# A two-block transformer kernel on one core: a fixed opening order with strided copies on three engines, and a norm summed by matmuls with its residual scaling put off

## Chip, cores and metric

One core of one Trainium2 chip. The metric is the device time of one execution in microseconds, as the median over several runs. The kernel is given all inputs in device memory and writes one 512 x 1024 output.

## The reference, cut to what matters

A first block (one Conformer-like layer with sparse attention) is followed by a second block of two attention layers. 512 tokens, width 1024, fp32 throughout. The change touches three places: the first block's first norm and the projections that follow it, the hand-over between the blocks (the first block's last sum and final norm, the second block's first norm), and the latent inputs and dense attention of the second block's first layer.

```python
def first_block(x, ...):
    h = rms_norm(x, norm1_g[l])                       # the opening
    proj = h @ w_in[l]                                # q, k_c, v_c, k_s, v_s, k_w, v_w, gates, ...
    ...                                               # compress(): windows of 32 tokens, step 16, of k_c and v_c
    x = x + (g_a * y_attn + g_b * y_conv) @ w_out[l]
    x = x + conv_ffn(rms_norm(x, norm2_g[l]), ...)    # its last product is ... @ w_down
    return rms_norm(x, final_g)                       # the residual x of the second block

def second_block(x, c, ...):
    for layer in range(2):
        shift, scale, gate = split(silu(c) @ ada_w[layer] + ada_b[layer])
        h = rms_norm_2(x, norm_w[layer]) * (1 + scale) + shift
        y = even_mixer(h, ...) if layer == 0 else odd_mixer(h, ...)
        x = x + gate * y
    return rms_norm_2(x, final_norm)

def even_mixer(h, ...):
    qa, ka, va, ga, cq, ckv, kr, gb = split(h @ w_in)
    oa = dense_gqa_attention(rope(rms_norm_2(qa)), rope(rms_norm_2(ka)), va)   # 8 heads, 512 x 512 scores
    cq, ckv = rms_norm_2(cq), rms_norm_2(ckv)                                  # the latent inputs
    ob = mla_attention(...)
    return concat([oa * silu(ga), ob * silu(gb)]) @ w_out
```

## The kernel before, in words

The residual is held transposed, as eight tiles X[k] of 128 channels x 512 tokens. Every fp32 operand of a large product is split into a rounded high part and a low remainder, and `mm3` (L121 to L126) makes three matmuls for each of them: L124 low by high, L125 high by low, L126 high by high. A weight tile is loaded by `wload` (L100): a DMA, ACT's copy to the high part (L110) and a subtraction for the low part (L111) on POOL or DVE. Results go to PSUM banks of four groups: "pg" and "ps" (two banks each), "pt" (three) and "po" (one). `gemm_bank` gives a pg bank, `wide_bank` pg and ps in turn. A tile framework adds the semaphores and a scheduler sets each engine's order from the dependences; where `in_order(engine)` stands around code, that engine takes those instructions in the order in which they are written.

Opening (L303 to L424). For each of the eight tiles ACT makes the high part, scaled by the gain (L305), and DVE the low part. Two key/value tiles pkv (24 matmuls each) follow, and eight squares on ACT with DVE adds between them (`Squares`, L193), summed over the partitions by eight fp32 matmuls with a one-column operand (L224, L225). `newton` makes the reciprocal root in eight small DVE steps (L164 to L173), and `row_bcast` spreads it over the partitions by four matmuls (L184), copied to R1 by DVE (L190). `windows` (L328) multiplies a pkv tile by R1 (L330), splits it (L152 on ACT, L153 on DVE) and lays it out as overlapping windows with 16 strided copies of 64 partitions x 8 x 31 elements, source step 16: eight of the high part on DVE (L347), eight of the low part on ACT (L349). It runs twice, for ZK and ZV. Two more tiles, pkb, are computed in between, multiplied by R1 (L402) and stacked by `stack_k` (L241 and L243 on ACT, L242 and L244 on DVE). Then `natural` (L405) computes four 280-column tiles wv in pg banks, each evacuated by ACT with the per-row factor (L417), and the query and compression products follow.

Hand-over (L755 to L806, L895 to L898). The last down product comes in two token halves th, of 256 columns: for each of the eight row tiles m a product of 12 matmuls in a wide bank, an add into X[m] on DVE (L792), and two squares on ACT: of X and of X times the final gain, each kind accumulated on DVE (L207, L210). At the end of a half: eight fp32 sum matmuls (L224, L225), Newton on four columns, a broadcast (L184), and for each k the modulated input by `modulated`: L772 on DVE, L773 on ACT, L774 on DVE. The split of w_kv and w_qa begins after the first half. After both halves, POOL turns X into the second block's residual with two instructions for each tile and half: times r0 (L897), times the final gain (L898). The program has them after the q/k/v products; POOL takes them where the scheduler lets them.

Latent inputs (`latent_inputs`, L881): four 416-column tiles in pg banks, each with its own squares and its own Newton before ACT's scaled copies can free the bank. Dense attention (`dense_scores`, L916): for each of eight heads, four score tiles, reduce_max on DVE (L924), Exp on ACT (L926), reciprocal on DVE (L927), and the scaling of P on POOL (L928); transposes of P and the product with the values follow. The gate and latent products of the loop take their weights through ACT L110 and POOL L111.

## Time and profile before

| | us |
|---|---|
| median of 3 runs (lowest, highest) | 1329.89 (1329.7, 1336.98) |
| profiled execution, its own time | 1332.08 |
| span of that execution | 1330.3 |
| PE busy in the span | 1259.4 |
| DVE, POOL, ACT busy | 930.5, 722.3, 707.0 |

The profile was taken from one execution; its own time is 1.8 us over its span and 2.2 us over the median of the runs. Times in the rows below are microseconds from the start of the span, unless marked ns. Engines: PE = TensorE matmuls, PEld = its weight loads (which run beside matmuls), DVE = VectorE, ACT = ScalarE, POOL = GpSimd, SP = SyncE. L12 is line 12 of the kernel. PEclk is the granted clock of TensorE as a share of full speed. A bracket behind a row is the idle time of the engine before it, and what ended it. An fp32 matmul leaves two records. Tile names are by kind (x, h, p, ps), without their numbers.

### The profile page before, as it was taken

The numbers are of one execution on the slowest core, as the hardware profiler recorded it, in microseconds if no ns is written. First come the engines' busy times: TensorE is split into PE (matmuls) and PEld (weight loads), VectorE is DVE, ScalarE is ACT, GpSimd is POOL, SyncE is SP. The second block draws the span as 40 slices with busy tenths as digits, with TensorE's granted clock in tenths as the row PEclk, the third lists the DMA queues.
The fourth block names the chain that finished last, engine by engine and source line by source line (L and its number), as shares of the span: only waits on it lengthen the run. The fifth ranks groups of instructions, "written<-read, shape, count | busy, mean of one in ns | idle before, by whom it ended". The sixth has DMA issues, their size and how long they took to land. (4 is left out here: it accounts for less than half of the span.)

```text
span 1330.3 us, 19304 instructions
## 1 busy us (share of the span) xinstructions
PE 1259.4 (95%) x6337; PEld 1044.6 (79%) x6337; DVE 930.5 (70%) x2042; ACT 707.0 (53%) x1497; POOL 722.3 (54%) x699
## 2 busy tenths in 40 slices
PE   7889999899999999999999979899999989999997
PEld 5778877688878888888888778878777788888886
DVE  7555666886644777754778788686788786666565
ACT  5736678434443444423443353386666645776554
POOL 4157786844644666655664554345445432767542
PEclk9899999999999999999999989999999989999998
DMA  7131112232333455555554601211111111111221
GB/s 228 40 100 48 49 50 65 89 101 88 119 111 95 159 170 163 165 187 164 170 158 131 221 24 39 62 46 46 45 55 48 33 56 48 60 59 52 70 72 64
DMA packets 71973, 124.75 MB, mean 94 GB/s; under 512 B 8257, under 2 KB 17345, under 8 KB 71873
## 3 DMA queue, kind: packets, MB, share of 16 engines
q1 hardware_dynamic: 71872, 123.52, 29.7%
q8 instruction: 50, 0.82, 0.2%
q14 instruction: 51, 0.41, 0.1%
HBM read 121.39 MB, written 2.10 MB: 93 GB/s over the span
## 5 line engine op out<-in xcount | busy, mean ns | idle before, releaser
L111 POOL TENSOR_TENSOR wl<-wr,wh 128x512 fp32r<-128x512 f32 (+2 forms) x215 | 286.3, 1333 | 283.4 <-ACT wh L110 224.5
L124 PE MATMUL pg<-h,wl 128*128 128x512 f32 x628 | 249.1, 397 | 3.2 <-POOL wl L111 3.1
L125 PE MATMUL pg<-h,wh 128*128 128x512 f32 x628 | 247.0, 393 | 0.0
L126 PE MATMUL pg<-h,wh 128*128 128x512 f32 x628 | 246.9, 393 | 0.0
L110 ACT ACTIVATE wh<-wr 128x512 fp32r<-128x512 f32 (+2 forms) x215 | 132.5, 618 | 157.3 <-PE pg L126 79.3
L124 PEld LDWEIGHTS pg<-h,wl 128*128 128x128 f32 x628 | 118.3, 188 | 26.9 <-POOL wl L111 4.5
L126 PEld LDWEIGHTS pg<-h,wh 128*128 128x128 f32 x628 | 118.4, 189 | 22.5
L125 PEld LDWEIGHTS pg<-h,wh 128*128 128x128 f32 x628 | 118.5, 189 | 22.4 <-issue 0.7
L111 POOL TENSOR_TENSOR m<-t,m 128x512 fp32r<-128x512 f32 (+1 forms) x67 | 87.9, 1312 | 75.2 <-ACT m L110 66.8
L286 PE MATMUL po<-t,h 128*128 128x512 f32 (+3 forms) x384 | 111.1, 365 | 7.5 <-DVE t L281 3.6
L281 DVE TENSOR_TENSOR t<-pt,t 128x512 fp32r<-128x512 f32 (+1 forms) x160 | 97.6, 631 | 28.3 <-ACT t L280 27.2
L124 PE MATMUL ps<-h,wl 128*128 128x512 f32 x260 | 103.7, 399 | 5.7 <-POOL wl L111 3.8
L125 PE MATMUL ps<-h,wh 128*128 128x512 f32 x260 | 102.6, 395 | 0.5 <-DVE h L156 0.5
L126 PE MATMUL ps<-h,wh 128*128 128x512 f32 x260 | 102.7, 395 | 0.0
L280 ACT ACTIVATE t<-pt 128x512 fp32r<-128x512 f32 (+1 forms) x160 | 84.4, 552 | 20.0 <-PE pt L276 19.3
L286 PEld LDWEIGHTS po<-t,h 128*128 128x128 f32 x384 | 65.7, 188 | 33.5 <-ACT t L280 16.4
L276 PE MATMUL pt<-k,p 128*128 128x128 f32 x576 | 86.6, 273 | 0.9 <-POOL p L928 0.7
L276 PEld LDWEIGHTS pt<-k,p 128*128 128x128 f32 x576 | 69.4, 140 | 13.7 <-POOL p L928 3.5
L928 POOL TENSOR_SCALAR p<-p,s 128x512 f32<-128x512 f32 x64 | 44.9, 704 | 62.9 <-DVE s L927 62.3
L702 DVE CUSTOM_DVE_ANT_0 b<-b,z 128x512 f32<-128x512 f32 x48 | 75.7, 1578 | 0.6 <-DMA b<-ada_t 0.6
L110 ACT ACTIVATE m<-t 128x512 fp32r<-128x512 f32 (+2 forms) x78 | 46.8, 602 | 40.3 <-PE ps L124 12.2
L124 PEld LDWEIGHTS ps<-h,wl 128*128 128x128 f32 x260 | 49.7, 191 | 17.8 <-POOL wl L111 4.8
(376 smaller groups left out, 3113.2 us busy)
## 6 DMA issues: line engine op xcount, KB each, us to landing
b<-ada_t SPq DMA_DIRECT2D x48, 256.0 KB, 3.1
z<-ada_t SPq DMA_DIRECT2D x48, 256.0 KB, 3.0
t<-w_up SPq DMA_DIRECT2D x44, 256.0 KB, 2.8
wr<-w_up SPq DMA_DIRECT2D x44, 256.0 KB, 2.7
wr<-w_g SPq DMA_DIRECT2D x32, 256.0 KB, 2.6
t<-w_dn SPq DMA_DIRECT2D x23, 256.0 KB, 2.8
wr<-w_br SPq DMA_DIRECT2D x16, 256.0 KB, 2.6
wr<-w_gt SPq DMA_DIRECT2D x16, 256.0 KB, 2.8
```

Source lines behind the costliest of these rows:

```text
L110: A.activation(hi[:, :z], raw[:, :z], AF.Copy)
L111: eng.tensor_sub(lo[:, :z], raw[:, :z], f(hi[:, :z]))
L124: PE.matmul(ps, ll, rh, start=start and i == 0, stop=False)
L125: PE.matmul(ps, lh, rl, start=False, stop=False)
L126: PE.matmul(ps, lh, rh, start=False, stop=stop and i == n - 1)
L276: PE.transpose(ps[:, o:o + 128], src, ident)
L280: evac[:] = [A.activation(hi[:, :n], ps[:, :n], AF.Copy)]
L281: evac.append(V.tensor_sub(lo[:, :n], ps[:, :n], f(hi[:, :n])))
L286: PE.matmul(o[:, a:b], v, t[:, pa:pa + b - a], start=start and z == 0, stop=stop and z == 1)
L702: V.tensor_tensor_reduce(out=raw, in0=raw, in1=CA[z], op0=OP.mult, op1=OP.add, scale=1.0, scalar=0.0, accum_out=MA[l][:, z, m:m + 1])
L928: G.tensor_scalar(p, p, sm[:, 1:2], 0.0, op0=OP.mult, op1=OP.add)
```

## The change

1. Opening. The high parts of all eight tiles, with their weights', now stand on ACT before the squares, in fixed order. PE's order is fixed as well: both pkv products, half of the first pkb product, the norm's sums (in a pt bank), its other half, the broadcast of R1, the second pkb product. Both pkv tiles are multiplied by R1 at once. The strided copies of each window set go four to DVE, six to ACT and six to POOL (before: eight, eight, none), and the products of pkb with R1 stand between the two window sets. The wv tiles take wide banks.
2. Second block's first norm. A class `Weighted` replaces the two `Squares` of a half: one square per row tile on ACT and no DVE adds, then, for both 128-token parts, an fp32 matmul of the squares with two columns (one, and the squared gain), accumulated in the "po" bank over the eight row tiles.
3. The factor on the queries, q3, moves from DVE to POOL.
4. The latent inputs take wide banks, and one Newton on eight columns serves all four tiles.
5. The residual's scaling moves from the hand-over into the dense loop: after each head's last scaling of P, the four POOL instructions of one tile X[k].

```diff
-        def sums(self):
-            st = new("ps")
+        def sums(self, bank="ps"):
+            st = new(bank)
...
+    class Weighted:
+        def __init__(self, a, w):
+            self.c, self.w, self.n, self.st = slice(a, a + 256), w, 0, new("po")
+        def add(self, src):
+            t = new("p")
+            A.activation(t[:, self.c], src[:, self.c], AF.Square)
+            k = self.n
+            for i in range(2):
+                PE.matmul(self.st[:, 2 * i:2 * i + 2], t[:, self.c][:, i * 128:(i + 1) * 128], self.w[:, k, :],
+                          start=k == 0 and i == 0, stop=k == KT - 1, skip_group_check=True)
+            self.n += 1
...
+    with in_order("PE"):
+        for b in range(2):
+            mm3(pkv[b], w0[8 * b:8 * b + 8], xg)
+        mm3(pkb[0], wk[0][:4], xg[:4], True, False)
+        r1 = rsqrt(total.sums("pt"), 1.0 / D, EPS)
+        mm3(pkb[0], wk[0][4:], xg[4:], False, True)
+        R1 = to_sbuf(row_bcast(r1, "pt"))
+        pkb.append(new("ps"))
+        mm3(pkb[1], wk[1], xg)
...
-                        if zz is zh:
+                        if zz is zh and o == 0:
                             V.tensor_copy(dst, src)
+                        elif zz is zh or g + o == 2:
+                            A.activation(dst, src, AF.Copy)
                         else:
-                            A.activation(dst, src, AF.Copy)
+                            G.tensor_copy(dst, src)
...
-        ps = natural(wv, xg, 280, i)
+        ps = natural(wv, xg, 280, i, wide_bank)
...
     def down(th, m, ps, c):
+        if m == 0:
+            sums.append(Weighted(256 * th, fg2))
         V.tensor_add(X[m][:, c], X[m][:, c], ps)
-        sums[th][0].add(X[m])
-        sums[th][1].add(X[m], cv("fg", m))
+        sums[th].add(X[m])
...
-                V.tensor_tensor(q3, q3, r[:, 0:8].to_broadcast([128, 8, 64]), op=OP.mult)
+                G.tensor_tensor(q3, q3, r[:, 0:8].to_broadcast([128, 8, 64]), op=OP.mult)
...
-    for r0, c in xr:
-        for k in range(KT):
-            G.tensor_mul(X[k][:, c], X[k][:, c], r0)
-            G.tensor_scalar(X[k][:, c], X[k][:, c], cv("fg", k), 0.0, op0=OP.mult, op1=OP.add)
-    for i in range(4):
-        latent_inputs(wc, i)
+    def latent_inputs(w):
+        ss = new("s", (128, 16))[:, 0:8]
+        banks = []
+        for i in range(4):
+            ps = natural(w, H, 416, i, wide_bank)
...
+        rc = rsqrt(ss, 1.0, EPS)
+        for i, ps in enumerate(banks):
...
+    def residual(k):
+        with tc.issue_after(getattr(scaled[0], "ins", scaled[0])):
+            for r0, c in xr:
+                G.tensor_mul(X[k][:, c], X[k][:, c], r0)
+                G.tensor_scalar(X[k][:, c], X[k][:, c], cv("fg", k), 0.0, op0=OP.mult, op1=OP.add)
...
         dense_output(h, P, [v[:, h // 4, :] for v in VA])
+        residual(h)
```

The order of the instructions at three places follows, before and after; the line numbers are each kernel's own.

ACT in the opening, before, from the split of the first pkv tile (p99) on: L349 are the strided copies, L361 a compression weight.

```order
L152 ACTIVATE p98_368<-p97_366 128x512
L349 ACTIVATE h101_373<-p99_369 64x8x31 x4
L349 ACTIVATE h103_387<-p99_369 64x8x31 x4
L152 ACTIVATE p105_402<-p104_400 128x512
L110 ACTIVATE wh141_651<-t140_650 128x512
L361 ACTIVATE wh149_691<-t148_690 128x2x128
L349 ACTIVATE h108_407<-p106_403 64x8x31 x4
L349 ACTIVATE h110_421<-p106_403 64x8x31 x4
```

The same place on ACT after the change (L376 are the strided copies, L390 the compression weights, L257 the first of the stack copies).

```order
L152 ACTIVATE p101_420<-p72_360 128x512
L376 ACTIVATE h103_424<-p101_420 64x8x31 x2
L376 ACTIVATE h105_438<-p101_420 64x8x31
L376 ACTIVATE h104_425<-p102_421 64x8x31
L376 ACTIVATE h105_438<-p101_420 64x8x31
L376 ACTIVATE h106_439<-p102_421 64x8x31
L390 ACTIVATE wh149_691<-t148_690 128x2x128
L390 ACTIVATE wl151_700<-wr150_699 128x2x128
L257 ACTIVATE h115_488<-p107_452 64x512
```

Six of the sixteen copies of a set stay on ACT between the split and the stack copies; six more are POOL's and four DVE's.

DVE where the first half's norm is applied while the second half's products arrive, before: L792 is the add into a row tile x, L774 the low part of a modulated input, L207 and L210 the adds of squares, L111 a weight split.

```order
L774 SCALAR_TENSOR_TENSOR h1889_7747<-p1887_7745,k1089_4351,h1888_7746 128x256
L792 TENSOR_TENSOR x7_112<-x7_112,pg1943_7893 128x256
L774 SCALAR_TENSOR_TENSOR h1892_7753<-p1890_7751,k1089_4351,h1891_7752 128x256
L207 TENSOR_TENSOR z1940_7887<-p1933_7849,p1936_7867 128x256
L774 SCALAR_TENSOR_TENSOR h1895_7759<-p1893_7757,k1089_4351,h1894_7758 128x256
L207 TENSOR_TENSOR z1942_7891<-p1934_7851,p1937_7869 128x256
L792 TENSOR_TENSOR x8_113<-x8_113,ps1946_7913 128x256
```

The same place after the change: L802 is the low part, L825 the add into a row tile.

```order
L802 SCALAR_TENSOR_TENSOR h1879_7727<-p1877_7725,k1089_4351,h1878_7726 128x256
L825 TENSOR_TENSOR x7_112<-x7_112,pg1929_7870 128x256
L802 SCALAR_TENSOR_TENSOR h1882_7733<-p1880_7731,k1089_4351,h1881_7732 128x256
L825 TENSOR_TENSOR x8_113<-x8_113,ps1931_7888 128x256
L802 SCALAR_TENSOR_TENSOR h1885_7739<-p1883_7737,k1089_4351,h1884_7738 128x256
L825 TENSOR_TENSOR x9_114<-x9_114,pg1933_7906 128x256
```

The adds of squares are gone from between; the add into x7 still stands behind the sixth of the eight low parts.

POOL in the dense loop before, around the end of one head's scalings (L928 scales P, L111 is a weight split for a gate product).

```order
L928 TENSOR_SCALAR p2125_8784<-p2125_8784,s2124_8782 128x512
L928 TENSOR_SCALAR p2129_8794<-p2129_8794,s2128_8792 128x512
L111 TENSOR_TENSOR wl2274_9277<-wr2272_9275,wh2273_9276 128x512
L928 TENSOR_SCALAR p2133_8804<-p2133_8804,s2132_8802 128x512
L928 TENSOR_SCALAR p2168_8943<-p2168_8943,s2167_8941 128x512
```

POOL in the dense loop after the change, at the end of another head's scalings (L960 scales P, L970 and L971 are the residual's two steps on tile x4, L111 is a weight split for a gate product).

```order
L960 TENSOR_SCALAR p2100_8690<-p2100_8690,s2099_8688 128x512
L970 TENSOR_TENSOR x4_109<-x4_109,r1861_7693 128x256
L970 TENSOR_TENSOR x4_109<-x4_109,r1944_7980 128x256
L971 TENSOR_SCALAR x4_109<-x4_109,k2_107 128x256 x2
L111 TENSOR_TENSOR wl2241_9175<-wr2239_9173,wh2240_9174 128x512
L960 TENSOR_SCALAR p2135_8833<-p2135_8833,s2134_8831 128x512
```

Four instructions now stand between a head's last P scaling and what follows it, a weight split here; before, scalings and splits alone made up the queue.

## Rows read from the trace of the kernel before

**Rows 1.** The page's first section: engines' busy time.
```profile
PE 1259.4 (95%) x6337; PEld 1044.6 (79%) x6337; DVE 930.5 (70%) x2042; ACT 707.0 (53%) x1497; POOL 722.3 (54%) x699
```

**Rows 2.** Windows: us, busy PE, PEld, DVE, ACT, POOL, PEclk, DMA, GB/s.
```profile
51.27:55.63 4.36, 4.36 (x18) 4.36 (x19) 2.13 (x5) 2.19 (x8) 1.60 (x2) 0.50 0.31 90
...
59.57:110.00 50.43, 45.93 (x245) 38.63 (x244) 29.19 (x79) 23.33 (x58) 25.45 (x28) 0.97 0.24 77
...
783.55:799.50 15.95, 8.66 (x40) 8.16 (x39) 15.95 (x25) 10.77 (x26) 12.03 (x14) 0.59 0.09 23
...
842.42:866.58 24.16, 18.34 (x91) 16.74 (x90) 14.34 (x61) 9.35 (x28) 2.58 (x2) 0.93 0.10 33
...
866.58:1000.00 133.42, 127.67 (x642) 99.76 (x640) 101.40 (x217) 94.41 (x209) 66.89 (x74) 1.00 0.15 46
```

**Rows 3.** Timeline of PE, opening: start, duration, instruction, idle before.
```profile
28.08 1.68 PE L184 MATMUL pt<-k,s 128*128 128x128 f32 x8 [2.27 <-DVE s L173]
...
39.57 0.29 PE L124 MATMUL pg<-m,h 128*128 128x280 f32 x1
...
51.27 0.60 PE L124 MATMUL pg<-m,h 128*128 128x280 f32 x1 [5.40 <-ACT p L417]
...
59.57 0.39 PE L124 MATMUL pg<-h,wl 128*128 128x512 f32 x1
```

**Rows 4.** Groups by form, 20 to 60 us: busy, mean ns, idle.
```profile
L349 ACT ACTIVATE h<-p 64x248 fp32r<-64x248 f32 x16 | 10.2, 638 | 1.6 <-DVE p L153 1.4
...
L347 DVE CAST h<-p 64x248 fp32r<-64x248 f32 x16 | 7.1, 441 | 0.2
...
L243 ACT ACTIVATE h<-p 64x512 fp32r<-64x512 f32 x4 | 2.5, 628 | 0.1
```

**Rows 5.** Timeline of ACT, opening.
```profile
33.71 5.17 ACT L349 ACTIVATE h<-p 64x248 fp32r<-64x248 f32 x8 [1.44 <-DVE p L153]
...
50.72 0.49 ACT L417 ACTIVATE p<-pg,s 128x280 f32<-128x280 f32 x1
```

**Rows 6.** Timeline of DVE, opening.
```profile
30.52 0.69 DVE L330 TENSOR_TENSOR p<-pg,r 128x512 f32<-128x512 f32 x1
```

**Rows 7.** Timeline of PE, hand-over and latent inputs.
```profile
787.21 0.58 PE L124 MATMUL pg<-h,h 128*128 128x256 f32 x1 [3.38 <-DVE x L792]
...
794.05 0.58 PE L124 MATMUL pg<-m,h 128*128 128x256 f32 x1 [3.91 <-DVE x L792]
...
846.85 0.43 PE L124 MATMUL pg<-m,h 128*128 128x416 f32 x1 [4.42 <-DVE p L833]
...
866.16 0.66 PE L906 MATMUL pt<-k,h 128*128 128x128 f32 x4 [1.40 <-ACT h L243]
```

**Rows 8.** Groups by form, 758 to 866 us.
```profile
L897 POOL TENSOR_TENSOR x<-x,r 128x256 f32<-128x256 f32 x16 | 12.7, 793 | 11.8 <-DVE p L772 11.8
...
L898 POOL TENSOR_SCALAR x<-x,k 128x256 f32<-128x256 f32 x16 | 9.0, 561 | 1.6
...
L210 DVE TENSOR_TENSOR z<-z,p 128x256 f32<-128x256 f32 x20 | 10.8, 562 | 1.3 <-ACT p L217 1.1
...
L224 PE MATMUL ps<-k,z 128*128 128x1 f32 x16 | 2.8, 246 | 0.0
```

**Rows 9.** Timeline of DVE, hand-over.
```profile
779.71 0.48 DVE L774 SCALAR_TENSOR_TENSOR h<-p,k,h 128x256 fp32r<-128x256 f32 x1
...
781.84 1.02 DVE L774 SCALAR_TENSOR_TENSOR h<-p,k,h 128x256 fp32r<-128x256 f32 x1
```

**Rows 10.** Timeline of POOL, hand-over.
```profile
781.84 0.74 POOL L897 TENSOR_TENSOR x<-x,r 128x256 f32<-128x256 f32 x1
```

**Rows 11.** The page's section of groups: two groups of POOL.
```profile
L111 POOL TENSOR_TENSOR wl<-wr,wh 128x512 fp32r<-128x512 f32 (+2 forms) x215 | 286.3, 1333 | 283.4 <-ACT wh L110 224.5
...
L928 POOL TENSOR_SCALAR p<-p,s 128x512 f32<-128x512 f32 x64 | 44.9, 704 | 62.9 <-DVE s L927 62.3
```

More of the change, by code (lines that the diff above doesn't have):

```diff
@@ L325, in gemm, with windows @@
         return ps
-    def windows(ps, pe):
-        t = new("p")
-        V.tensor_mul(t, ps, R1)
+    def windows(t, pe):
         th, tl = split(t, p="p")
@@ L387, in build @@
     KB = []
-    wk = [wsplit(I["w_q"][2 + b], KT, 128) for b in range(2)]
     wv = wsplit(I["w_v"], KT, 280, ("m", "h"))
@@ L395, in build @@
     w2k, w2v = [(w2h[:, i:i + 64], w2l[:, i:i + 64]) for i in (0, 64)]
-    ZK = windows(pkv[0], cv("pek", 0, 16))
-    ZV = windows(pkv[1], cv("pev", 0, 16))
+    ZK = windows(tkv[0], cv("pek", 0, 16))
+    tkb = []
     for b in range(2):
-        ps = new("ps")
-        mm3(ps, wk[b], xg)
-        t = new("p")
-        V.tensor_mul(t, ps, R1)
+        tkb.append(new("p"))
+        V.tensor_mul(tkb[b], pkb[b], R1)
+    ZV = windows(tkv[1], cv("pev", 0, 16))
+    for t in tkb:
         KB.append([stack_k(t, 0), stack_k(t, 64)])
@@ L788, in build @@
     H = [None] * KT
-    sums = [[Squares(256 * th, 256 * th + 256) for _ in range(2)] for th in range(2)]
+    fg2 = new("k", (128, KT, 2), tag="fg2")
+    V.memset(fg2[:, :, 0], 1.0)
+    V.tensor_mul(fg2[:, :, 1], cv("fg", 0, 8), cv("fg", 0, 8))
+    sums = []
     def down(th, m, ps, c):
+        if m == 0:
+            sums.append(Weighted(256 * th, fg2))
         V.tensor_add(X[m][:, c], X[m][:, c], ps)
-        sums[th][0].add(X[m])
-        sums[th][1].add(X[m], cv("fg", m))
+        sums[th].add(X[m])
     xr = []
@@ L927, in dense_scores @@
             V.reciprocal(sm[:, 1:2], sm[:, 0:1])
-            G.tensor_scalar(p, p, sm[:, 1:2], 0.0, op0=OP.mult, op1=OP.add)
+            scaled[0] = G.tensor_scalar(p, p, sm[:, 1:2], 0.0, op0=OP.mult, op1=OP.add)
             P.append(p)
         return P
+    scaled = [None]
+    def residual(k):
[3 more added lines that the diff above has]
+                G.tensor_scalar(X[k][:, c], X[k][:, c], cv("fg", k), 0.0, op0=OP.mult, op1=OP.add)
     def dense_values(h, P, vs, dst):
```

71 lines of the change are left out of this document (37 added, 34 removed).

## The prediction

> **What bounds the kernel now.** I read the engines' busy time first. TensorE is busy 1259.4 us of a 1330.3 us span, 95%, and no other engine is above 70% [rows 1]. So a change gains only where TensorE stands still or runs at the lower of its two levels (1.2 instead of 2.4 GHz, a granted clock of 0.50 instead of 1.00), and it costs only where it adds work to TensorE or makes it wait. I then asked, in the timeline of TensorE, for the idle time in front of its matmuls at the places that the change touches, and in windows for the granted clock behind them.
>
> The opening has one long stop. The second pkb product is done and the first two wv tiles run from 39.57 us on; then TensorE waits 5.40 us for L417, ACT's evacuation of the first wv tile, and goes on at 51.27 [rows 3]. Until 55.63 its clock is 0.50, with all 4.36 us busy [rows 2]. The query product starts at 59.57 [rows 3]. L417 is late because of ACT's queue: from 33.71 on it holds sixteen strided copies at 638 ns and eight stack copies at 628 ns, and reaches L417 at 50.72 [rows 4, 5]. An earlier stop of 2.27 us, for Newton's last step in front of the broadcast of R1 [rows 3], stays: the chain of sums, Newton and broadcast is the same.
>
> The hand-over has two stops, 3.38 us before 787.21 and 3.91 us before 794.05, both for DVE's add into X, L792 [rows 7]. Between 783.55 and 799.50 TensorE is busy 8.66 of 15.95 us, at a mean clock of 0.59, while DVE is busy for all of it [rows 2]. DVE is the bound there. The latent inputs have a stop of 4.42 us for one tile's own Newton and rope (L833), and one of 1.40 us behind them [rows 7]; the clock of that window is 0.93 [rows 2]. In the dense loop TensorE is busy 127.67 of 133.42 us at full clock, and POOL 66.89 [rows 2].
>
> **The opening.** What goes: the wait of 5.40, and the lower clock behind it, under which 4.36 us of work would have taken 2.18. Together 7.6 us. It goes for two reasons. The wv tiles take four banks in turn instead of two, so the third tile no longer waits for L417. And ACT has 12 strided copies instead of 16 in front of L417, 4 x 638 ns = 2.6 us less, so L417 comes at about 48. What is late next: the query product needs the bank of the second wv tile. Two tiles took 51.27 - 5.40 - 39.57 = 6.3 us, so four take 12.6, and TensorE asks for that bank near 52; ACT has some 3 us in hand. The new fixed order puts the squares behind the high parts, which should let the pkv products end somewhat sooner; the sums then come somewhat later behind half of pkb. I set these against each other, at nothing.
>
> What it adds: 12 strided copies on POOL, a form that POOL does not show. From the nearest rows, the scaling of 128 x 512 at 704 ns is 0.34 us for 248 elements, and a whole two-input instruction is 1.33 us [rows 11]. DVE takes 0.44 and ACT 0.64 for the same copy [rows 4]. I take 0.64, ACT's row being of the same shape. A set of six is then 4 us, and even at 1.33 it is 8 us; both sets end before 55, and their reader, the compression, stands behind the query product. So the copies as such hide. Their possible harm is to DVE, and through it to TensorE: the wv tiles now need the pkb banks, which the products with R1 free on DVE, and these stand behind the first set's four casts. DVE starts R1's products at 30.52 [rows 6]; two products at 0.69, a split of about 1, four casts at 0.44 and the first pkb product of 0.69 end near 35.6, before the first wv tile wants its bank. Opening: 7.6 us gained, between 2.6 (rival A) and 8.6, if all that I set at nothing turns out well by 1 us.
>
> **The hand-over.** What goes: the waits of 3.38 + 3.91 = 7.3 us, and the lower clock from 787.21 to 799.50: 12.29 less the wait of 3.91 inside it is 8.4 us of work at the lower level, worth 4.2. Together 11.5. DVE's chain shrinks by more than one thing. POOL's 32 residual instructions leave (12.7 + 9.0 = 21.7 us of POOL [rows 8]). While they ran, L774 took 1.02 us, against 0.48 before they began [rows 9], and the longer one began together with an L897 [rows 10]. Eight low parts at 0.54 less are 4.3 us. And the adds of squares, 562 ns each [rows 8], leave the gaps between the adds into X: two stand before x8, two more before x9, together 2.2. That is 6.5 us on DVE against stops of 7.3, so a remainder of about 1 us is left as a wait, L825 on x7 still standing behind the sixth low part. The w_qa splits, which could take POOL's place beside the low parts, need ACT's copies first, and those are queued behind the modulated high parts; so I expect L774's short duration.
>
> The Trainium skill, page "SBUF — State Buffer", section "Who interferes with whom", has the rule behind this: DVE and GpSimd share one port pair as an exclusive lock, and a DVE instruction with two SBUF inputs contends with a GpSimd instruction that reads SBUF. The trace agrees, with 1.02 beside L897 and 0.48 without. By the same rule the opening's copies on POOL speak against the change, since DVE's splits run beside them (rival A).
>
> What it adds on TensorE: the eight small sums of a half, in pairs of matmuls, become sixteen, one pair for each row tile, so 16 more instructions over both halves. A record of this form takes 246 ns and an instruction has two [rows 8]: between 0.25 us each, if one hides the other, and 0.49, so 4.0 to 7.9 us. I take 4.0, the matmuls being issued between long runs of others. Sum: 11.5 - 4.0 - 1.0 = 6.5 us gained. Bounds: 1 (rival B), and 9.5, if sums fall partly into waits and nothing remains of the stops. q3 on POOL is four instructions of twice L897's width, some 1.6 us each at most; their readers, the transposes, come behind the four latent products, so they cost nothing.
>
> **The latent inputs.** Removed: 4.42, the lower clock behind it (0.07 of 24.16, 1.7 us) and, if the stack copies come while the products still run, the 1.40: 7.5 us. Added: the next gate product must wait until the one Newton and the scaled copies free a bank. The nearest row is the same Newton's stop of 2.27 in the opening [rows 3]; with an ACT copy of 0.63 [rows 4] that is 2.9, and the lower clock again 1.7. Gain 2.9, with ends 0 (the new stop as long as the old) and 7.5 (hidden behind the transposes).
>
> **The dense loop.** Each head gets 2 x 0.793 + 2 x 0.561 = 2.7 us more on POOL [rows 8], eight times, 21.7 us. POOL goes from 66.89 to about 88.6 of 133.42 us, 66%. Queued behind them are the next weight split and the next head's P scalings, for which TensorE's transposes wait. A head is 133.42 / 8 = 16.7 us, POOL free for about half of it, and the scalings of the next head are made one head ahead of their use. I charge 1 us, with ends 0 and 39 (rival C). DVE's reads of the scores are from PSUM, so I expect no slower DVE there.
>
> **Sum.** 7.6 + 6.5 + 2.9 - 1.0 = 16.0 us. The profiled execution took 1332.08, so 1316.1 for such a one; the median of the runs lies 2.2 lower, and so the forecast is 1314.0 us.
>
> **The rivals.** A: the copies on POOL hold DVE in the opening. Speaking for it is L774's doubling beside POOL [rows 9, 10], and that these strided reads are unlike anything POOL does here; against it, that DVE has over 1 us in hand before the first pkb bank is wanted. If each of DVE's four casts waits out a copy of 1.33 us, 4 x 0.89 = 3.6 us are added, TensorE stops about 2.8 us and runs 2.2 us longer at the lower level: 5 us of the gain go, 1319.0 us. A sentence apart: the Trainium skill, page "GPSIMD Engine Reference", section "Performance pitfalls for Q7 kernels", says that reads with a byte step over 8 cost about 2.9 cycles per element; with that page's 1.2 GHz an estimate of 0.6 us per copy, which no run here shows, and by which the sum would stay as it is.
>
> B: in the hand-over POOL's weight splits move onto the place of L897 and L898, at 1.33 us each [rows 11], and L774 stays at 1.02. Then 4.3 us stay on DVE, TensorE still stops and falls to the lower level, and of 6.5 only 1 is left: 1319.5 us. For it: those splits are next in POOL's queue. Against: they wait for ACT.
>
> C, slower: POOL in the dense loop has no room where it matters. If the four instructions stand exactly in front of the scaling or split that TensorE needs next, each head stops for 2.7 us, with 2.2 us for the lower level behind it as at 51.27: 8 x 4.9 = 39 us in place of 1, and 1352 us. It decides once the order leaves POOL less than 2.7 us of slack in front of what TensorE needs; when the stops come to 17 us in all, 2.1 us a head, the whole gain is gone. For it: the order puts them in front of a weight split. Against: TensorE's idle time there is 5.75 us in all, with POOL busy only half the time.
>
> D: the opening's gain is given back. The work after it gets its weights no sooner, and TensorE waits for splits between 59.57 and 110 instead. For it: there are 4.5 us of idle time in that window already; against: the DMA share is 0.24, POOL half busy [rows 2]. Price 7.6: 1321.6 us.
>
> **How the numbers follow.** Forecast 0.60, A 0.13, B 0.13, C 0.05, D 0.06, something dearer 0.03. The forecast's own range is 1307 to 1319, from the ends of sums, latents and loop that are not rivals. A measurement of this kernel tells about 1% from no change, so faster means under 1316.6. Of the forecast's 0.60 some 0.52 lies there, and of A and B, which may come mildly, 0.08: 0.60. The rest of these and D give 0.33 within 1%, C and part of the last case 0.07 slower. The range runs from 1305 (both bounds above in the hand-over and the latents in part) to 1322 (D), and leaves C out.
>
> **What would show it.** Right: no wait for the wv evacuation, the query product at about 52 us instead of 59.57; the low part of the modulated input near 0.48 us in the first half; no stop over 1.5 us for the add into X and a granted clock near 1.00 through the second half; one stop of about 3 us in front of the first gate product; POOL near 89 us busy in the dense loop with TensorE's idle time there below 8 us. Wrong: a TensorE stop for a pkb bank near 37 us (A), L802 near 1 us beside L111 (B), a stop for the P scaling or a weight split in every head (C), new waits for weights between 52 and 110 us (D).

## The result and the profile after

| | before | changed |
|---|---|---|
| median of 16 runs (lowest, highest), us | 1330.67 (1328.87, 1336.98) | 1323.47 (1320.57, 1328.22) |
| ratio of the two, 95% interval | | 0.9949 [0.9941, 0.9958] |
| profiled execution, its own time, us | 1332.08 | 1324.7 |
| span of it, us | 1330.3 | 1322.9 |

The change is worth 0.5%, some 7 us, where 16 were forecast, and it lies outside the range. The direction was right; less than half of the size came.

To see where, the program is cut at three matmuls that both kernels have: the first product of the hand-over (256 columns), the first latent product (416 columns) and the first score product of the dense loop. Their starts are read off TensorE's timeline.

| stage | before, us | changed, us | difference | forecast |
|---|---|---|---|---|
| start to hand-over | 758.64 | 751.41 | -7.2 | -7.6 |
| hand-over | 74.55 | 76.42 | **+1.9** | **-6.5** |
| latent inputs, transposes | 33.39 | 30.51 | -2.9 | -2.9 |
| dense loop to the end | 463.7 | 464.6 | +0.8 | +1.0 |

Three of four terms came out to within half a microsecond, not all of them for the reasons given (see below). The whole miss is the hand-over. The engines' busy time, for [rows 1]:

```profile
PE 1256.7 (95%) x6369; PEld 1044.3 (79%) x6369; DVE 908.1 (69%) x1981; ACT 697.4 (53%) x1477; POOL 731.1 (55%) x715
```

DVE lost 22 us of work and TensorE 3, and still the hand-over grew. TensorE's timeline of the changed kernel shows its stops, to be held against [rows 3, 7].

```profile
32.91 1.71 PE L184 MATMUL pt<-k,s 128*128 128x128 f32 x8 [4.17 <-DVE s L173]
...
53.27 0.39 PE L124 MATMUL pg<-h,wl 128*128 128x512 f32 x1
...
757.34 1.01 PE L241 MATMUL po<-k,p 128*128 128x2 f32 x4 [3.26 <-ACT p L237]
...
780.24 1.54 PE L184 MATMUL pt<-k,s 128*128 128x128 f32 x8 [2.01 <-DVE s L173]
...
851.41 0.47 PE L124 MATMUL pg<-h,wl 128*128 128x512 f32 x1 [4.20 <-DVE p L866]
```

The 5.40 us of the opening are gone and the query product starts at 53.27 instead of 59.57. The two stops for the add into X are gone too. In their place stand one of 3.26 us, in front of the first sum matmul of the first half, which waits for ACT's square, and one of 2.01 in front of the broadcast, for Newton's last step (0.39 before). Windows of the changed kernel, with the columns of [rows 2], show the clock behind each:

```profile
59.57:110.00 50.43, 45.49 (x255) 37.94 (x253) 31.52 (x93) 25.29 (x64) 30.42 (x33) 1.00 0.27 86
...
757.00:763.80 6.80, 6.46 (x30) 6.46 (x31) 0.84 (x2) 1.12 (x3) 0.00 (x0) 0.50 0.06 23
780.90:784.30 3.40, 3.40 (x18) 3.40 (x17) 2.07 (x6) 1.70 (x4) 0.00 (x0) 0.50 0.03 12
...
858.34:1000.00 141.66, 133.87 (x674) 105.33 (x673) 108.04 (x225) 98.17 (x218) 89.71 (x110) 1.00 0.16 51
```

Behind each of the two new stops the clock is 0.50: 6.46 us of work cost 3.2 more than at full clock, 3.40 us cost 1.7. With the stops, 3.3 + 3.2 + 2.0 + 1.7 = 10.2 us. That is the reading with which the experiments began. (The two clocks are those of this one execution: in the run e2 below the same stop for Newton is followed by full clock.)

Why does the first square come late? The answer stands in DVE's and ACT's queues ahead of it.

```profile
751.35 0.69 DVE L730 CUSTOM_DVE_ANT_0 b<-b,z 128x512 f32<-128x512 f32 x1 [1.32 <-DMA b<-ada_t]
...
754.63 0.69 DVE L111 TENSOR_TENSOR z<-wr,z 128x512 fp32r<-128x512 f32 x1 [2.59 <-ACT z L110]
...
755.83 0.68 DVE L780 TENSOR_TENSOR x<-x,pg 128x512 f32<-128x512 f32 x1
756.42 0.41 DVE L825 TENSOR_TENSOR x<-x,ps 128x256 f32<-128x256 f32 x1
```

```profile
753.97 0.63 ACT L110 ACTIVATE z<-wr 128x512 fp32r<-128x512 f32 x1 [9.87 <-DMA wr<-w_qa]
756.87 0.42 ACT L237 ACTIVATE p<-x 128x256 f32<-128x256 f32 x1 [2.27 <-DVE x L825]
```

DVE's part of one w_qa split, not wanted for another 45 us, stands ahead of the add into X. It waits 2.59 us for ACT's copy, and that for its DMA. The add comes at 756.42, the square at 756.87. TensorE had the first product done near 753 and nine matmuls of the second by 754.08; next in its queue stands the sum of that square. In the kernel before, the order has this split behind three of the adds:

```
L752 TENSOR_TENSOR x11_116<-x11_116,pg1819_7460 128x512
L792 TENSOR_TENSOR x4_109<-x4_109,ps1823_7495 128x256
L792 TENSOR_TENSOR x5_110<-x5_110,pg1826_7513 128x256
L207 TENSOR_TENSOR z1831_7547<-p1824_7509,p1827_7527 128x256
L207 TENSOR_TENSOR z1833_7551<-p1825_7511,p1828_7529 128x256
L792 TENSOR_TENSOR x6_111<-x6_111,ps1829_7531 128x256
L111 TENSOR_TENSOR z1916_7801<-wr1914_7799,z1915_7800 128x512
```

In front of the adds it would have hurt less there, as far as the order tells (no run shows it): the sums came at the end of the half, and only the four banks in turn tied TensorE to the adds.

### The profile page after: what moved, and what is told of

It reads as the page before. It is cut to its first block, busy times and chain, and to the rows that moved or that the text cites. A ratio compares the mean times of both kernels' runs of the same rounds, so it can differ in the third digit from the quotient of the medians.

```text
span 1322.9 us, 19282 instructions
## 1 busy us (share of the span) xinstructions
PE 1256.7 (95%) x6369; PEld 1044.3 (79%) x6369; DVE 908.1 (69%) x1981; ACT 697.4 (53%) x1477; POOL 731.1 (55%) x715
## 4 chain that ended last, share of the span: by engine, by line
PE 76%; DVE 9%; ACT 5%; POOL 3%; issue 3%; DMA 2%; SPq 0%; DVEq 0%; ACTq 0%; POOLq 0%
PE pg L124 13%; PE pg L126 13%; PE pg L125 13%; PE ps L124 7%; PE ps L125 7%; PE ps L126 7%; PE po L302 5%; PE pt L292 3%; PE ps L953 2%; PE ps L1148 2%; POOL h L478 1%; POOL wl L111 1%; PE ps L563 1%; DVE z L210 1%; DMA x<-xT 1%
## 5 line engine op out<-in xcount | busy, mean ns | idle before, releaser
L111 POOL TENSOR_TENSOR wl<-wr,wh 128x512 fp32r<-128x512 f32 (+2 forms) x215 | 286.4, 1334 | 268.7 <-ACT wh L110 210.5
L111 POOL TENSOR_TENSOR m<-t,m 128x512 fp32r<-128x512 f32 (+1 forms) x67 | 87.7, 1310 | 81.3 <-ACT m L110 75.2
L960 POOL TENSOR_SCALAR p<-p,s 128x512 f32<-128x512 f32 x64 | 44.8, 704 | 59.4 <-DVE s L959 58.8
L124 PE MATMUL pg<-h,m 128*128 128x512 f32 (+1 forms) x144 | 57.2, 397 | 7.3 <-DVE m L111 7.3
```

The lines of the kernel that those rows point to most:

```text
L111: eng.tensor_sub(lo[:, :z], raw[:, :z], f(hi[:, :z]))
L124: PE.matmul(ps, ll, rh, start=start and i == 0, stop=False)
L960: scaled[0] = G.tensor_scalar(p, p, sm[:, 1:2], 0.0, op0=OP.mult, op1=OP.add)
```

## The experiments

Each run is compared with runs of the kernel before on the same chip. Differences to the changed kernel are differences of these ratios (the changed kernel's is 0.9949), times 1330 us. Lines in the rows are those of each kernel's own file.

**e1_lag: the sums held back.**

```diff
...
             A.activation(t[:, self.c], src[:, self.c], AF.Square)
-            k = self.n
+            self.held.append(t)
+            if len(self.held) > 4:
+                self.sum()
+
+        def sum(self):
+            t, k = self.held.pop(0), self.n
             for i in range(2):
                 PE.matmul(self.st[:, 2 * i:2 * i + 2], ...)
...
+        while sums[th].held:
+            sums[th].sum()
         st = sums[th].st[:, 0:4].rearrange("p (i z) -> p z i", z=2)
```

> The changed kernel, with the sum matmuls of each row tile held back until four more tiles have been squared; nothing is left out. In the changed kernel TensorE stops 3.26 us for the first square (L241 behind L237) and then has about 6.8 us at the lower clock, worth 3.2. Theory S (the sums put TensorE's queue behind DVE's add and ACT's square of the first tile): stop and lower clock go, 4 to 6.5 us faster than the changed kernel. Rival B (TensorE would stop there anyway, for a bank that the late add frees): a stop for L825 of 2 us or more takes its place, within 1 us of the changed kernel. Rival M (what the first norm lost is the 16 extra sum matmuls themselves): no more than 1 us faster.

Measured: 1320.51 us, ratio 0.9922 [0.9906, 0.9939], 3.6 us faster than the changed kernel. The stop at the first square is gone. Windows of this kernel: the hand-over, and the stretch that was at the lower clock.

```profile
752.42:820.99 68.57, 66.40 (x466) 61.66 (x465) 48.50 (x132) 27.05 (x63) 19.89 (x18) 1.00 0.16 45
757.00:764.00 7.00, 7.00 (x61) 7.00 (x62) 2.29 (x7) 2.33 (x6) 0.00 (x0) 1.00 0.09 31
```

The hand-over takes 68.57 instead of 76.42 us, all at full clock. The stop for Newton is shorter too, 1.1 instead of 2.0 us, and no lower clock stands behind it; with 0.6 us for the square of a later tile and 0.4 for an add, both in the second half, 2.1 us of stops are left. No stop of 2 us for a bank took the old one's place, so rival B of this run falls, and with the sums all still there, rival M does too. The time gained is a little under what was expected, and less than the 7.9 us of the stage. In the two profiled executions, 1.0 us of the rest is lost ahead of the hand-over, which starts at 752.42 instead of 751.41. Another 1.4 us is lost much later: after a stop of 2.5 us for the sums of a later norm, the same stretch of TensorE's work took 8.11 us at a clock of 0.58 here (the first row) and 6.74 us at 0.75 in the changed kernel (the second row).

```profile
1066.02:1074.13 8.11, 8.11 (x43) 8.11 (x44) 3.78 (x14) 1.46 (x4) 2.50 (x2) 0.58 0.34 110
```

```profile
1072.68:1079.42 6.74, 6.74 (x43) 6.60 (x44) 4.50 (x14) 1.47 (x4) 2.50 (x2) 0.75 0.45 133
```

Just before, in the attention's output product, both kernels stop 0.57 and 1.00 us for adds. The second stop was followed by a clock of 0.60 here (the first row) and of 1.00 in the changed kernel (the second row). That difference cost next to nothing, because the changed kernel then waits 1.16 us for a weight split.

```profile
1055.75:1060.00 4.25, 4.25 (x23) 4.25 (x24) 3.21 (x7) 3.02 (x8) 1.51 (x2) 0.60 0.00 0
```

```profile
1062.51:1066.00 3.49, 3.12 (x24) 2.92 (x24) 3.21 (x7) 3.03 (x8) 1.32 (x1) 1.00 0.00 0
```

**e2_wqa_behind_adds: the split moved behind four adds.**

```diff
-        V.tensor_add(X[m][:, c], X[m][:, c], ps)
+        adds.append(V.tensor_add(X[m][:, c], X[m][:, c], ps))
...
-            wqa = wsplit(I["w_qa"], KT, 512, ...)
+            with tc.issue_after(getattr(adds[3], "ins", adds[3])):
+                wqa = wsplit(I["w_qa"], KT, 512, ...)
```

> The changed kernel, with DVE's part of the w_qa splits queued behind the fourth add into X of the first half (by the order, one DVE instruction moves, from ahead of the last full-width add and the first L825 to behind three of them); nothing is left out. Theory S: the first add is late because this split waits 2.6 us on DVE for a weight's DMA; without it the add comes some 1.5 us sooner, the stop of 3.26 us shrinks to 1 to 2 us, and the kernel is 1.5 to 5 us faster than the changed one, depending on whether the lower clock goes too. Rival (the stop has its cause ahead of DVE's queue, in the last products of the tile before): the stop stays above 2.5 us and the time within 1 us.

Measured: 1320.32 us, 0.9919 [0.9904, 0.9934], 4.0 us faster. The waits of TensorE in the hand-over of this kernel (in total, how many, the longest):

```profile
PE pt L184 <- DVE s L173: 2.0, 1, 2.0
PE po L241 <- ACT p L237: 1.2, 1, 1.2
```

One instruction moved on one engine took two thirds of the stop for the square. The stop for Newton is as long as in the changed kernel, and yet no stretch at the lower clock is left, not even behind it; the hand-over takes 70.45 us. The work behind Newton's stop in this run:

```profile
778.90:782.30 3.40, 3.40 (x31) 3.40 (x30) 2.92 (x8) 2.26 (x6) 0.00 (x0) 1.00 0.00 0
```

The rival falls: the cause was in DVE's queue.

**e3_newton_alone: POOL's splits away from Newton.**

```diff
-        A.activation(r0, R[:, 0:256], AF.Copy)
+        r0c = A.activation(r0, R[:, 0:256], AF.Copy)
...
-            wkv = wsplit(I["w_kv"], KT, 256, ("m", "m"))
+            with tc.issue_after(getattr(r0c, "ins", r0c)):
+                wkv = wsplit(I["w_kv"], KT, 256, ("m", "m"))
```

> The changed kernel, with ACT's part of the four w_kv splits queued behind the copy of r0 of the first half, so that no weight split of POOL runs beside the first Newton; nothing is left out. In the changed kernel two of Newton's steps took 1.26 and 1.22 us, each begun together with a POOL split, others 0.16, and TensorE stopped 2.01 us in front of the broadcast. Theory P (POOL's splits hold DVE's small steps): both steps fall below 0.3 us, the stop falls below 0.6 us. The splits then run beside the modulated low parts, which should grow from 0.48 towards 1.0 us; 0 to 3.5 us faster than the changed kernel if that costs less than it saves. Rival (small DVE steps are slow by themselves or wait for each other): the stop stays near 2 us.

Measured: 1327.82 us, 0.9972 [0.9958, 0.9986], 3 us slower than the changed kernel, where 0 to 3.5 us faster was expected. Newton came out as theory P has it. In the changed kernel, DVE and POOL at the first Newton:

```profile
775.79 1.26 DVE L164 TENSOR_SCALAR s<-s 128x4 int32<-128x4 int32 x1
777.09 0.16 DVE L167 TENSOR_TENSOR s<-s 128x4 f32<-128x4 f32 x1
...
778.77 1.22 DVE L172 SCALAR_TENSOR_TENSOR s<-s 128x4 f32<-128x4 f32 x1
```

```profile
775.75 1.29 POOL L111 TENSOR_TENSOR m<-t,m 128x512 fp32r<-128x512 f32 x1 [22.18 <-ACT m L110]
778.61 1.35 POOL L111 TENSOR_TENSOR m<-t,m 128x512 fp32r<-128x512 f32 x1 [1.58 <-ACT m L110]
```

Each long step began within 0.2 us of a POOL split and ended with it. In this run every step took 0.15 to 0.17 us and the stop was gone. (So was the stop at the first square, since the w_qa copies moved with the others.) But the splits now run beside the modulated low parts:

```profile
780.07 1.49 DVE L802 SCALAR_TENSOR_TENSOR h<-p,k,h 128x256 fp32r<-128x256 f32 x1
781.49 0.41 DVE L825 TENSOR_TENSOR x<-x,pg 128x256 f32<-128x256 f32 x1
781.82 1.44 DVE L802 SCALAR_TENSOR_TENSOR h<-p,k,h 128x256 fp32r<-128x256 f32 x1
```

```profile
779.74 1.54 POOL L111 TENSOR_TENSOR m<-t,m 128x512 fp32r<-128x512 f32 x1 [27.77 <-ACT m L110]
781.70 1.28 POOL L111 TENSOR_TENSOR m<-t,m 128x512 fp32r<-128x512 f32 x1 [0.42 <-ACT m L110]
```

Two low parts take 1.49 and 1.44 us instead of 0.48, DVE's own splits grow as well, and TensorE stops 2.1 and 1.8 us for the adds. This is rival B of the prediction, brought about by the order of this run: its mechanism is real, but the changed kernel's order did not bring it about. Where the 3 us are lost is not shown. In the profiled execution the hand-over takes 75.45 us, 1.0 less than in the changed kernel, because the two old stops are gone; its span is 0.8 us longer.

**e4_opening_of_before: the other parts without the opening.** The edit puts the opening's functions of the kernel before (the loop that loads X, `windows`, the pkb products, the wv banks) back into the changed kernel.

```diff
-    total = Squares()
-    with in_order("Activation"):
...
+    pkv = []
+    for b in range(2):
+        pkv.append(gemm_bank())
+        mm3(pkv[b], w0[8 * b:8 * b + 8], xg)
...
-        ps = natural(wv, xg, 280, i, wide_bank)
+        ps = natural(wv, xg, 280, i)
```

> The changed kernel with the opening (order, strided copies, wv banks) of the kernel before; nothing is left out. If the opening's gain is kept to the end and the hand-over is late for reasons of its own, this is 7.0 us slower than the changed kernel, so about as slow as the kernel before (1329 to 1332 us), and the stop for the first square is still there, 2.5 us or more. Rival E (the hand-over stops because the earlier start runs into weights that arrive no sooner): the stop for the first square is under 1 us and this kernel is only 1 to 4 us slower than the changed one.

Measured: 1330.58 us, 0.9988 [0.9974, 1.0001], 5 us slower than the changed kernel and no different from the kernel before. The two intervals leave room for the 7.0 expected. The stop for the first square is there, but at 1.9 us, where 2.5 or more was expected and the changed kernel has 3.26. So rival E of this run holds in part. ACT's copy of the w_qa weight in this run:

```profile
759.24 0.63 ACT L110 ACTIVATE z<-wr 128x512 fp32r<-128x512 f32 x1 [9.48 <-DMA wr<-w_qa]
```

The hand-over starts at 758.05 here and the copy 1.2 us later; in the changed kernel it starts at 751.41 and the copy 2.6 us later. The hand-over came 6.6 us sooner, its weight 5.3, and the 1.4 us between them is the difference of the two stops. For the rest the opening's gain is kept, and the other four parts together are worth nothing that can be told from zero; rival D of the prediction falls.

**f1_squares_back: without the sums by matmul.** `Weighted` is taken out and the two `Squares` of a half come back, the residual stays put off.

```diff
-        if m == 0:
-            sums.append(Weighted(256 * th, fg2))
         V.tensor_add(X[m][:, c], X[m][:, c], ps)
-        sums[th].add(X[m])
+        sums[th][0].add(X[m])
+        sums[th][1].add(X[m], cv("fg", m))
```

> The changed kernel with the two Squares of a half back in place of Weighted (two squares per row tile, DVE adds, eight sum matmuls at the end of a half); the residual stays put off, nothing is left out. Theory S (in the changed kernel the per-tile sum matmuls put TensorE behind DVE's first add): no stop at the first square, the hand-over (first half's first product to first latent product) falls from 76.4 to 70 plus or minus 2 us, and the kernel is 3 to 6 us faster than the changed one. Rival D (DVE's adds of squares are what held the adds into X): stops for L825 in the second half of 3 us or more in all, hand-over at 74 us or more, within 2 us of the changed kernel or slower.

Measured: 1323.63 us, 0.9950 [0.9931, 0.9969], the same as the changed kernel. Its single runs spread from 1317.44 to 1329.14. The hand-over is 73.3 us, between the two expectations. The waits of TensorE there:

```profile
PE ps L224 <- DVE z L210: 2.6, 2, 2.3
PE pg L124 <- DVE x L820: 2.4, 2, 1.7
PE pt L184 <- DVE s L173: 0.4, 1, 0.4
```

No stop at the first square, as theory S has it; but the adds of squares hold TensorE instead, for the sums at the end and for the adds into X. The sums by matmul, as the change has them, swap one set of stops for another of the same size (5.3 and 5.4 us). The run undoes two things at once, though: with the squares back, DVE's order has the w_qa split behind three of the adds again (at 756.85 us; the adds are at 754.17, 754.50 and 756.51). So the split came to the front together with the new form of the sums, and it is e1 and e2, not this run, that tell the two apart.

The run also prices the sums. The hand-over of the changed kernel (first row) and of this run (second row), at the same mean clock:

```profile
751.41:827.83 76.42, 71.14 (x466) 66.26 (x465) 47.59 (x132) 27.29 (x63) 19.51 (x18) 0.93 0.14 39
```

```profile
751.39:824.67 73.28, 67.86 (x433) 62.63 (x432) 59.12 (x156) 33.05 (x79) 21.25 (x18) 0.93 0.14 39
```

TensorE is busy 3.3 us longer with the 16 more instructions.

**f2_residual_alone: the kernel before with only the residual put off.**

```diff
-    for r0, c in xr:
-        for k in range(KT):
-            G.tensor_mul(X[k][:, c], X[k][:, c], r0)
-            G.tensor_scalar(X[k][:, c], X[k][:, c], cv("fg", k), 0.0, op0=OP.mult, op1=OP.add)
...
         dense_output(h, P, [v[:, h // 4, :] for v in VA])
+        residual(h)
```

> The kernel before with the residual's scaling put off into the dense loop and nothing else changed; nothing is left out. Theory P (POOL's residual instructions hold DVE's low parts, and that causes the two stops for the add into X): L774 near 0.48 us in the first half, the stops of 3.38 and 3.91 us shrink to under 2 us together, the hand-over falls from 74.5 to about 67 to 69 us, of which the dense loop gives back about 1: 4 to 7 us faster than before. Rival B (weight splits take POOL's place beside the low parts, or the adds of squares alone hold DVE): stops of 4 us or more remain, under 2 us faster than before.

Measured: 1329.0 us, 0.9994 [0.998, 1.0008]: no difference. L774 does fall to its short duration (the first row: mean over both halves 481 ns, 739 before), and the stops for the add into X shrink from 7.3 to 2.4 us. The hand-over takes 72.27 us in the profiled execution, 2.3 less than before. But there is a new stop of 2.3 us for the sums of squares (L224, for L210), POOL's w_qa splits come up behind, and an add of squares, L210, takes 1.19 us beside them:

```profile
L774 DVE SCALAR_TENSOR_TENSOR h<-p,k,h 128x256 fp32r<-128x256 f32 x16 | 7.3, 481 | 0.0
```

```profile
786.22 0.70 DVE L111 TENSOR_TENSOR h<-wr,h 128x512 fp32r<-128x512 f32 x1
786.82 0.77 DVE L210 TENSOR_TENSOR z<-z,p 128x256 f32<-128x256 f32 x2
787.49 0.43 DVE L792 TENSOR_TENSOR x<-x,pg 128x256 f32<-128x256 f32 x1
787.82 1.19 DVE L210 TENSOR_TENSOR z<-z,p 128x256 f32<-128x256 f32 x1
```

```profile
786.79 6.51 POOL L111 TENSOR_TENSOR h<-t,h 128x512 fp32r<-128x512 f32 x4 [7.76 <-ACT h L110]
```

So both expectations are half right: the contended low parts were the cause of the two stops, and the next POOL work takes over as soon as they are free, on the adds. Only with the adds gone too (the sums by matmul) does the second half run without a stop, as in the changed kernel.

**f3_opening_newton: the opening's Newton without POOL beside it.** In `query_pair`; `first[0]` is ACT's copy in the first split of `windows`.

```diff
-        ps = gemm(I["w_q"][4 + m], xg)
+        if m == 0:
+            with tc.issue_after(getattr(first[0], "ins", first[0])):
+                ps = gemm(I["w_q"][4 + m], xg)
+        else:
+            ps = gemm(I["w_q"][4 + m], xg)
```

> The changed kernel, with ACT's copies of the first query weights queued behind the first split of the windows, so that POOL's two splits of them no longer run beside the opening's Newton; nothing is left out. In the changed kernel Newton's steps ran from about 27 to 32.8 us, with two small steps of 1.22 and 1.32 us beside POOL splits, and TensorE stopped 4.17 us. Theory P: no small step over 0.8 us, the stop falls to 2 to 3 us, the query product starts 1 to 2 us sooner than at 53.27, and the kernel is 1 to 2 us faster than the changed one if the query weights are still in time. Rival: the steps are late because of the small window instructions between them; the stop stays at 3.8 us or more.

Measured: 1321.83 us, 0.9937 [0.9918, 0.9955], 1.6 us faster than the changed kernel by the ratio, though the intervals overlap. In the trace it is plain: the stop in front of the broadcast is 2.1 us instead of 4.17, and the query product starts at 51.21 instead of 53.27. Newton's longest step is 0.74 us.

**f4_lag_and_wqa: both mends of the first square.** The edits of e1 and e2 together.

> The changed kernel with both the sums held back by four tiles and DVE's w_qa splits queued behind the fourth add into X; nothing is left out. Theory S: both act on the same stop, so together they give little more than either alone (4 us faster than the changed kernel): 4 to 6 us faster. Rival (they act on different losses, and add up): 7 us or more faster.

Measured: 1318.18 us, 0.9916 [0.9896, 0.9936], 4.4 us faster than the changed kernel, little more than either alone. They act on the same stop.

**g1_three_mended and g2_latents_in_pairs: a version that beats both.** g1 has the edits of e1, e2 and f3. g2 adds this:

```diff
-        for i in range(4):
-            ps = natural(w, H, 416, i, wide_bank)
...
-        rc = rsqrt(ss, 1.0, EPS)
+        for y in (0, 2):
+            ss = new("s", (128, 16))[:, 0:4]
+            for i in range(2):
+                ps = natural(w, H, 416, y + i, wide_bank)
...
+            rc = rsqrt(ss, 1.0, EPS)
```

> The changed kernel with three mends at once: sums held back by four tiles, DVE's w_qa splits behind the fourth add into X, and the first query weights' copies behind the first split of the windows; nothing is left out. If the stop for the first square and the longer stop of the opening's Newton are separate losses, their gains add: 5 plus 1.6, so 5.5 to 7.5 us faster than the changed kernel, a ratio to before of 0.989 to 0.991. If the opening's earlier start is eaten by weights arriving later in the hand-over: 4 to 5 us faster than the changed kernel, 0.9915 or more.

> The same three mends, and the latent inputs' Newton once for each pair of tiles instead of once for all four, so that the first pair's two banks come free while the second pair's products run; nothing is left out. Theory L (the stop of 4.2 us in front of the first gate product is the wait of its bank for the one Newton and the copies behind it): that stop falls under 1 us and the lower clock behind it goes, and the kernel is 3 to 6 us faster than with the three mends alone. Rival (the gate's bank is only where TensorE waits first, and the transposed latents or keys' stacks come late in any case): the stop moves to the score product or the transposes, under 1.5 us faster.

Measured: g1 1317.73 us, 0.9904 [0.9888, 0.9921], 6.0 us faster than the changed kernel. The gains of the opening and of the hand-over add up, as far as the intervals tell. g2 1311.34 us, 0.9859 [0.9844, 0.9873], another 6.0 us, and 1.4% under the kernel before. The wait for the gate's bank in g1 (first row, hand-over and latents) and what is left of it in g2 (second row):

```profile
PE pg L124 <- DVE p L884: 4.2, 1, 4.2
```

```profile
PE pt L957 <- ACT h L266: 1.6, 1, 1.6
```

The stop at the gate's bank is gone. One of 1.6 us stands instead at the transposes, for ACT's stacked queries, as the rival said, but it is short, and the stage falls from 30.6 to 27.6 us at full clock. That is 3.0 us, and so is the difference of the two profiled executions, 1317.33 and 1314.33 us. The medians differ by 6.4; the second half of that gain is not placed.

## Why the prediction was wrong, and where it was right

**The opening was right in its mechanism, and by luck in its last microsecond.** Forecast 7.6 us, measured 7.2 at the hand-over and 5 by e4, whose interval reaches from 2 to 8. The stop for the wv evacuation and the lower clock behind it went, as worked out. Two of the things set at nothing were not nothing: the sums start at 24.03 instead of 21.80 us, and Newton, with POOL's query splits beside it, holds TensorE 4.17 instead of 2.27 us, so the query product starts at 53.27 and not at 52, a gain of 6.3 us. What made up for it came later and is luck: the stretch at the lower clock between 59.57 and 110 [rows 2] did not come up in this execution, the clock there being 1.00. In other runs with the same opening it was 0.93 (e2 and e3), 0.97 (e1) or 1.00 (f1), and with the opening of before it was 1.00 in f2.

The copies on POOL were bounded well. Groups by form of the changed kernel, 20 to 60 us, against [rows 4]:

```profile
L378 POOL CAST h<-p 64x248 fp32r<-64x248 f32 x12 | 8.5, 707 | 6.8 <-DVE p L153 6.3
...
L376 ACT ACTIVATE h<-p 64x248 fp32r<-64x248 f32 x12 | 7.2, 634 | 0.1
...
L374 DVE CAST h<-p 64x248 fp32r<-64x248 f32 x8 | 5.0, 622 | 0.1
```

A copy takes 707 ns on POOL, where 640 was taken between 340 and 1330. Rival A's mechanism is there, mildly. The means of DVE's copies, 441 ns before and 622 after, hide its size; least, median and greatest duration (ns) of them, before and after, show it:

```profile
L347 DVE CAST h<-p x16: 359/372/1481, 33.6 to 44.0; 64x248 fp32r<-64x248 f32 x16
```

```profile
L374 DVE CAST h<-p x8: 359/708/717, 37.4 to 46.1; 64x248 fp32r<-64x248 f32 x8
```

Before, a copy took about 0.37 us, and the one of 1.48 us ran beside a weight split on POOL of 1.29. After, the first copy of each set began before POOL's and took 0.36 or 0.37 us; the other three ran beside POOL's and took about 0.71. A set costs DVE 1.0 us more than it would without POOL, and no stop for a pkb bank followed. The Trainium skill, page "GPSIMD Engine Reference", section "Performance pitfalls for Q7 kernels", gives reads with a byte step over 8 about 2.9 cycles per element, from which the prediction had its estimate of 0.6 us. The trace's 707 ns is 0.1 us over that estimate, and no run shows what the 0.1 is.

**The latent inputs and the dense loop came out at the forecast, in part by luck.** 2.9 and 0.8 us, against 2.9 and 1.0. The latents' terms do not add up to it: the new stop in front of the gate was put at 2.9 us and is 4.20, with a lower clock behind it that costs 1.7 as forecast:

```profile
851.41:858.34 6.93, 6.92 (x26) 5.39 (x26) 4.05 (x15) 4.57 (x10) 1.29 (x1) 0.75 0.00 1
```

With the 7.5 us that went, only 1.6 should be left; where the other 1.3 came from is not shown. g2 shows that this stop was not needed at all. In the loop POOL is busy 89.71 of 141.66 us, close to the 88.6 of the prediction, but that was for 133.42 us; in the first 133.42 us of the loop it is 83.24. TensorE's waits for a scaling of P grew from 0.7 to 1.1 us in all. Rival C falls. The 0.8 us itself says little: from the first score product to the end, the profiled executions of the runs with the same loop take between 464.4 and 466.6 us.

**The hand-over was wrong**, by 8.4 us. What the prediction removed went as it said: no stop for an add in the second half, and L802 at 0.48 us. What it added on TensorE was also of about the right size: the extra sums were put at 4.0 us, and f1 gives 3.3. With the forecast's own terms, 74.55 - 11.5 - 0.4 + 4.0 = 66.7 us is the bare stage (0.4 is Newton's stop before). The changed kernel's two new stops and their lower clock make 66.7 + 10.2 = 76.9, and 76.42 were measured; e1, with 2.1 us of stops left and no lower clock, should take 68.8, and took 68.57.

The step that failed is the sentence that costs the sums: "I take 4.0, the matmuls being issued between long runs of others." It took them as work alone. The sum matmuls also add a wait to TensorE's queue, in each of the sixteen places, for a square that hangs on DVE's add; and nothing was said of what stands ahead of that add on DVE. DVE's order had it plain: a w_qa split, moved from behind three adds to in front of the first. e1 takes the stop of 3.26 us away by moving the wait, and e2 two thirds of it by moving the split. By e4, 1.4 us of the 3.26 came only with the earlier start, for which the split's weight did not come as much sooner. The second step that failed is the silence on the first Newton: its cost was carried over from before, 0.39 us of stop, while the order put POOL's w_kv splits beside it. In the kernel before, one step ran beside such a split, and it took 1.02 us:

```profile
773.78 1.02 DVE L164 TENSOR_SCALAR s<-s 128x4 int32<-128x4 int32 x1
```

In the changed kernel two did, at 1.26 and 1.22 us. e3 shows the mechanism, and f3 shows the same in the opening.

Rival B was closer than its chance said, in kind if not in place: what took the gain back was contention with POOL's splits and a split's place in DVE's queue. With the residual alone put off (f2), the splits do move in, and the gain is zero: part 5 earns nothing by itself. Taking part 2 out of the changed kernel costs nothing (f1). Part 2 without part 5 was not run.

The Trainium skill, page "SBUF — State Buffer", section "Who interferes with whom", was used for the low parts only. Its rule speaks of a DVE instruction with two SBUF inputs and a GpSimd instruction that reads SBUF. L172, a step of that kind, agrees: it took 1.22 us beside a POOL split of 1.35, and 0.16 without. L164 has one tensor input and took 1.26 us beside a split of 1.29, so that sentence of the rule does not cover it.

Open: where e3 loses its 3 us and where half of g2's gain comes from; why f1 and e3 spread over 9 to 12 us from run to run where the kernel before spreads over 3 to 8; and a stop of 2.3 to 3.0 us for a weight split near 730 us, which the changed kernel and the runs share with the kernel before and which none of the edits touched.

## What to carry to other kernels

When sums move from the end of a loop into it, the tensor engine's queue gets a wait at every place; read, for the first of them, every instruction ahead of its producer in the producer's queue, DMA waits included, and hold the sums back by a few tiles if the producer may be late. Where a chain of tiny vector instructions gates the tensor engine, look what long GpSimd instruction can run beside it: each overlap here cost up to that instruction's whole length. A change of order can also bring a transfer's wait into the path by starting a stage sooner than its weights follow. And a stop that is taken away is worth its length plus the lower clock behind it only if no other stop is then followed by the lower clock instead.

## What the runs showed that was not expected

A DVE instruction of 128 x 4 elements takes 1.22 to 1.26 us instead of 0.16 when it begins just after a POOL split of 1.3 us has begun, and it ends with the split. A strided DVE copy of 64 x 248 elements takes about 0.71 us beside strided POOL copies, 0.37 without, and 1.48 beside a POOL split of 1.29. The same stop of 1.00 us in the attention's output was followed by a granted clock of 1.00 in one kernel and 0.60 in another that differed only some 300 us earlier, in one execution of each. The same stop of 2.01 us for Newton was followed by 0.50 in the changed kernel and by 1.00 in e2.
